# A hybrid decoder layer on one core: decay tiles clamped on ScalarE, running sums two ticks later, two mix tiles split together

## The chip, the core and the metric

The kernel runs on one core of a Trainium2 chip. A core has a matrix engine (PE, with its weight loads PEld), a vector engine (DVE), a scalar engine (ACT), GpSimd (POOL) and SyncE (SP, which here only issues DMAs). Each engine executes its own instructions in the order in which they are written, and waits on semaphores for the others. The metric is the device time of one execution in microseconds; the times shown are medians over several runs.

## The reference

One layer is computed for 256 tokens of width 1024, in float32:

```
p = x @ W_in -> [z | xBC | dt | q | k | v | gates]
s = Mamba-2 SSD mixer(z, conv(xBC), dt)      # 32 heads of 64, 4 groups, state 128
a = sliding-window attention with sinks(q, k, v)
m = (sig(g_s) * (s @ P_ssm) + sig(g_a) * (a @ P_attn)) @ W_o
h = LayerNorm1(alpha * x + m)
y = LayerNorm2(alpha * h + MoE(h))           # top 4 of 32 experts
```

The part that the change touches most is the decay inside one chunk of 128 tokens. With the running sums `a_cum = cumsum(dt * A)` of each head, it is

```
seg    = a_cum[:, :, :, None] - a_cum[:, :, None, :]
decay  = exp(where(causal, seg, -inf))
y_diag = einsum('bctgn,bcsgn->bctsg', C, B) * decay @ (x * dt)
```

## The kernel before, in words

**Front, 0 to 402 us.** All projections run here. Each weight tile is 128 x 2048 floats (1 MB). SP loads it into one of two ring slots (`load_raw`, L110). ACT copies it to a rounded high part (`act`, L67), DVE subtracts to get the low part (`sub_lo`, `tt`, L70), and PE makes three passes: high by high, high by low and low by high (`mm3`, L81). One half of a tile (128 output columns by 256 tokens) is 24 matmuls and one tick of the kernel's own clock. `take()` hands out the next tile; before that, `split_ahead` splits the tiles that come `st["la"]` places later: first the ACT copies, then all work that has fallen due (`run_due`), then the DVE subtractions. A ring slot is free again when the DVE subtraction has read it.

**Order of the side work.** `later(d, fn)` puts work d ticks ahead; generators that `yield need(d, ...)` are resumed when their tick has come and their counters allow. So the constants DT, DD and DE and the number in each `later` set where an instruction stands in its engine's queue. The tiles come in the order k, v, c8 to c11 (convolved B and C), then q0, c0, c1, q1, and so on, then z, the gates, the output projections and four mix tiles.

**Running sums.** `part_dt` issues `dt_product` (the dt projection), one tick later `dt_chain` (softplus by a series on DVE; result `av` = dt * A; transposes `pdn` at L404), DD ticks later `decays` (the sums `pacum` by matmul with triangles, then `acn`, `eac`, `dte` on ACT), and one tick after that `decay_rows`: PE transposes `acn` to `acT` (L515), ACT copies it and sends it to memory as `accd` (L518).

**Decay tiles.** `ssd(c, g)` runs for two chunks and four groups. It loads a tile E of 128 x 8 x 128 (the sums of 8 heads, spread over all partitions) from `accd` through POOL's queue (L525). For each head DVE subtracts that head's own sum and takes the minimum with zero (`ts`, L75, 8 instructions). One tick later ACT takes Exp of the whole tile; a tick after that DVE multiplies by the masked C-B product; then 16 matmuls per pair of groups form `yd` with E as their weights. `xs` and `xd` are scaled copies of the transposed conv output; their DVE instructions free the PSUM banks in which PE's `ws` sums go on.

**Mix and experts.** The last output projection tiles (`yss`) are gated into `m`; `mix(c, q)` multiplies by the four mix tiles. Then come LayerNorm 1, the router and, from 401.6 us, the experts: a stream of 2 MB tiles, issued by `prefetch` (L140) on SP into ten slots that the front's weight tiles use as well. An expert tile waits for its slot's last reader.

Of the kernel before, what the change touches and what calls it, by code (L numbers as in the profile page):

```python
# [11 lines left out]
AF = mybir.ActivationFunctionType  # L12
OP = mybir.AluOpType
AX = mybir.AxisListType

P = 128
# [15 lines left out]
SILU = "silu_and_others"  # L32
OVER, AL = 27, 7
BIAS = 12 * 18 + 4
DT, DD, DE = 2, 4, 2
D3 = 4
L1 = 2
LG, LS = 1, 1
# [6 lines left out]
def hybrid_layer(ctx, tc, x, w_in, conv_w, conv_b, dt_bias, a_log, d_skip, norm_w, w_ssm_out,  # L45
# [10 lines left out]
    def ptile(name, dt=F):  # L56
        return gran.tile([P, 4096], dt, name=name, tag="g")
# [5 lines left out]
    def bank(name):  # L63
        return psum.tile([P, 512], F, name=name, tag="bank")

    def act(o, i, func=AF.Copy, **kw):
        return nc.scalar.activation(o, i, func, **kw)  # L67

    def tt(o, a, b, op):
        return nc.vector.tensor_tensor(o, a, b, op=op)  # L70

    def ts(o, a, s1, s2, op0, op1=None):
        if op1 is None:
            return nc.vector.tensor_scalar(o, a, s1, None, op0=op0)  # L74
        return nc.vector.tensor_scalar(o, a, s1, s2, op0=op0, op1=op1)  # L75
# [4 lines left out]
    def mm(o, l, r, start, stop):  # L80
        return nc.tensor.matmul(o, l, r, start=start, stop=stop)  # L81
# [16 lines left out]
    st = {"dma": 0, "split": 0, "la": 1}  # L98
# [33 lines left out]
    def prefetch(upto):  # L132

        while moe[0] < min(upto, len(stream) - S_E):
            m = moe[0]
            ap, nb = stream[S_E + m]
            t = ptile(f"w{m}").rearrange("p (k n) -> p k n", n=nb)
            last = S_E + m == len(stream) - 1
            for ks in (slice(0, 2), slice(2, 3), slice(3, 4)) if last else (slice(0, 4096 // nb),):
                nc.sync.dma_start(t[:, ks], ap[:, ks])  # L140
            raws[S_E + m] = t
            moe[0] += 1
# [7 lines left out]
    def later(d, fn):  # L150
        due.setdefault(clock[0] + d, []).append(fn)
# [6 lines left out]
    def weights(i):  # L158

        prefetch_raw()  # L160
        split_ahead(i)
        prefetch_raw()
        nb = stream[i][1]
        return tuple(t.rearrange("p (k n) -> p k n", n=nb) for t in splits.pop(i))
# [67 lines left out]
    def w2(shape, name):  # L232
        return work.tile(shape, F, name=name, tag="w2", bufs=TB["w2"])

    def w4(shape, name):
        return work.tile(shape, F, name=name, tag="w4", bufs=TB["w4"])

    def sm(name, n=64, dt=F):
        return work.tile([P, n], dt, name=name, bufs=1)
# [65 lines left out]
    def need(d, when=None, **n):  # L305

        return clock[0] + d, when, n

    def done(**n):
        for k, v in n.items():  # L310
            left[k] += v
# [19 lines left out]
    def tick(end):  # L331
        clock[0] += 1
        if end:
            pend[0] = True
        else:
            run_due()
            side()

    def side():
        owed[0] = min(owed[0] + st.get("rate", 0), 4)  # L340
        while owed[0] >= 1 and advance():
            owed[0] -= 1

    def mm3(o, hi, lo, s, ah, al, first=True, last=True):

        for k in range(8):
            mm(o, hi[:, k, s], ah[:, k], first and k == 0, False)
            mm(o, hi[:, k, s], al[:, k], False, False)
        for k in range(8):
            mm(o, lo[:, k, s], ah[:, k], False, last and k == 7)  # L350
# [3 lines left out]
    def take():  # L354
        nxt[0] += 1
        w = weights(nxt[0] - 1)
        if pend[0]:
            pend[0] = False
            side()
        return w  # L360
# [26 lines left out]
    def dt_product():  # L387
        pdt = bank("pdt")
        for k in range(8):
            mm(pdt[0:32, 0:NT], wdth[:, k], xh[:, k], k == 0, False)  # L390
            mm(pdt[0:32, 0:NT], wdth[:, k], xl[:, k], False, False)
            mm(pdt[0:32, 0:NT], wdtl[:, k], xh[:, k], False, k == 7)
        pc = bank("pc")
        nc.tensor.transpose(pc[:, 0:120], cnat[0:120], ident[0:120, 0:120])
        nc.tensor.transpose(pc[:, 128:144], gnat, ident[0:16, 0:16])
        act(ccol[:, 0:120], pc[:, 0:120], scale=0.5)
        act(gcol, pc[:, 128:144], scale=0.5)
        ts(dtT, pdt[0:32, 0:NT], dtb[:, 0:1], None, OP.add)
# [80 lines left out]
    Bn, cbm, c1 = cb_t[:, 0], [cb_t[:, 1], cb_t[:, 2]], cb_t[:, 3]  # L479
# [20 lines left out]
    acn = sm("acn")  # L500
# [19 lines left out]
    def ssd(c, g):  # L520
        gcs = slice(512 * g, 512 * g + 512)
        yield need(0, w4=1, xe=1 - c)
        E = w4([P, 8, P], "E")
        r = 32 * c + 8 * g
        nc.gpsimd.dma_start(E, accd[r:r + 8].unsqueeze(0).to_broadcast([P, 8, P]))  # L525
        if c == 0:
            xe = w2([P, 512], "xe")
            nc.gpsimd.tensor_tensor(xe.rearrange("p (h d) -> p h d", d=64),
                                    xs[0][:, gcs].rearrange("p (h d) -> p h d", d=64),
                                    dte[:, 8 * g:8 * g + 8].unsqueeze(2).to_broadcast([P, 8, 64]), op=OP.mult)  # L530
        yield need(DE)
        for h in range(8):
            ts(E[:, h], E[:, h], acn[:, r + h:r + h + 1], 0.0, OP.subtract, OP.min)
        later(1, lambda: act(E, E, AF.Exp))
        later(2, lambda: tt(E, E, cbm[c][:, g, None, :].to_broadcast([P, 8, P]), OP.mult))
        yield need(1, (lambda: g in ready) if c else None, bank=1)
        if c == 0:
            pst = bank(f"st{g}")
            mm(pst, Bn[:, g], xe, True, True)

        else:
            po = bank(f"yo{g}")
            mm(po, c1[:, g], xs[0][:, gcs], True, True)

            def ev():
                tt(po.rearrange("p (h d) -> p h d", d=64), po.rearrange("p (h d) -> p h d", d=64),
                   eac[:, 8 * g:8 * g + 8].unsqueeze(2).to_broadcast([P, 8, 64]), OP.mult)
                tt(xd[1][:, gcs], po, xd[1][:, gcs], OP.add)
                done(bank=1)
            later(1, ev)  # L550
        yield need(2, bank=1)
        py = bank(f"yd{c}{g}")
        for h in range(8):
            mm(py[:, 64 * h:64 * h + 64], E[:, h], xs[c][:, 512 * g + 64 * h:512 * g + 64 * h + 64], True, True)

        def add_y():
            tt(xd[c][:, gcs], py, xd[c][:, gcs], OP.add)
            done(bank=1, w4=1)
            ready.add((c, g))
            if c == 0:  # L560
                act(xs[0][:, gcs], pst)
                later(1, lambda: ready.add(g))
                done(bank=1, xe=1)
        later(1, add_y)
# [146 lines left out]

    def part_dt():
        dt_product()
        later(1, dt_chain)
        later(DD, decays)
        later(DD + 1, decay_rows)

    for kind, j in ORDER:
        if kind == "c":
            conv(j)  # L720
            if j == 11:
                start(3, prep())
            elif j < 8 and j % 2:
                start(5, ssd(0, j // 2), ssd(1, j // 2))
# [71 lines left out]
    def bias_cols():  # L796
        pg = bank("pgu")
        for b in range(16):
            o = 512 * (b // 4 % 2) + b % 4
            nc.tensor.transpose(pg[:, 32 * b:32 * b + 32], bgn[b // 8][:, o:o + 509:4], ident[0:32, 0:32])  # L800
        pg3 = pg.rearrange("p (b e) -> p b e", e=32)
        act(bgu[:, 0:8], pg3[:, 0:8])
        ts(bgu[:, 8:16], pg3[:, 8:16], 1.0, None, OP.add)
# [3 lines left out]
    def merge(blk, ps):  # L807
        t = w1([P, NT], "mg")
        stt(t, gts[0][:, blk], 1.0, ps, OP.add, OP.mult)
        tt(mrg[:, blk], mrg[:, blk], t, OP.add)  # L810
        act(mh[:, blk], mrg[:, blk], scale=0.5)
        stt(ml[:, blk], mrg[:, blk], 0.5, mh[:, blk].bitcast(F), OP.mult, OP.subtract)

    st["la"] = LS
    for n in range(4):
        if n == 1:
            prefetch(2)
            nc.scalar.preload_act_table_set(EXP_LN)
        ps = [bank(f"yss{n}{b}")[:, 0:NT] for b in range(2)]
        for kh in range(2):  # L820
            hi, lo = take()
            if n == 3 and kh == 1:
                st["la"] = 2
            for b in range(2):
                mm3(ps[b], hi, lo, slice(b * P, (b + 1) * P), *yT[kh], kh == 0, kh == 1)
                if kh:
                    later(1, lambda b=b, n=n, ps=ps: merge(2 * n + b, ps[b]))
                tick(b == 1)
            if n == 0 and kh == 0:
                bias_cols()  # L830
# [417 lines left out]
    scale = []  # L1248
# [40 lines left out]
```

## Time and profile before

| | us |
|---|---|
| median of 3 runs | 1321.22 (1319.17 to 1322.77) |
| the profiled execution | 1322.42 |
| its span in the trace | 1320.6 |
| PE busy | 1242.5 (94%) |
| DVE busy | 432.7 (33%) |
| ACT busy | 282.7 (21%) |
| POOL busy | 22.3 (2%) |

The shares are means over two very different parts. In the front all of PE, DVE and ACT have much to do and wait for each other. In the expert stage, which takes two thirds of the span, DVE and ACT are nearly idle and the DMA share is about 1. A wait or a busy share is therefore to be read in its own stretch. PEclk is the clock that TensorE was granted, 1.00 being the upper of its two levels (2.4 GHz) and 0.5 the lower (1.2 GHz); a mean between them says that part of the stretch ran at each.

### The profile page before, as it was taken

What the parts mean: (1) busy time and instruction counts of PE and PEld (TensorE: products, weight loads), DVE (VectorE), ACT (ScalarE), POOL (GpSimd) and SP (SyncE); (2) the same over time, 40 slices, a digit from 0 to 9 for tenths busy, and PEclk for the clock granted to TensorE, in tenths of its full rate; (3) what the DMA queues carried; (4) which work ended last, traced back from release to release, by engine and by line L of the source; (5) the groups of instructions that cost most, each with busy time, mean ns of one, the idle gap of its engine ahead of it and who ended that gap; (6) DMA issues with size and microseconds to landing.
All of it is one profiled execution on the core that took longest, in us unless ns stands there. A gap on an engine that the chain in (4) does not pass through costs nothing. (4 is left out here: it accounts for less than half of the span.)

```text
span 1320.6 us, 16115 instructions
## 1 busy us (share of the span) xinstructions
PE 1242.5 (94%) x6835; PEld 676.4 (51%) x6835; DVE 432.7 (33%) x877; ACT 282.7 (21%) x471; POOL 22.3 (2%) x28
## 2 busy tenths in 40 slices
PE   7998899999999999999999999898999989879995
PEld 7997777999874343443433334243333424333331
DVE  4899878664651121112111121111111211111114
ACT  3655545653411110111100101010110101000001
POOL 0001101000000000000000000000000000000000
PEclk9999989999999999999999999999999999989998
DMA  6544345667598999999999999999999999999994
GB/s 207 161 154 157 115 140 188 224 219 276 191 430 337 430 430 431 431 430 430 431 429 430 432 429 430 432 430 429 431 432 428 431 431 430 431 426 431 431 429 173
DMA packets 80002, 467.49 MB, mean 354 GB/s; under 512 B 7052, under 2 KB 46164, under 8 KB 55220
## 3 DMA queue, kind: packets, MB, share of 16 engines
q1 hardware_dynamic: 78500, 460.99, 85.0%
q0 software_dynamic: 1200, 4.33, 0.9%
q8 instruction: 55, 0.90, 0.2%
q10 hardware_dynamic: 224, 1.08, 0.2%
q14 instruction: 23, 0.19, 0.0%
HBM read 465.30 MB, written 1.08 MB: 353 GB/s over the span
## 5 line engine op out<-in xcount | busy, mean ns | idle before, releaser
L81 PE MATMUL u<-w,xg 128*64 128x512 f32 x2048 | 462.5, 596 | 20.1 <-DMA w<-in_w_gate_up_dram 20.0
L81 PEld LDWEIGHTS u<-w,xg 128*64 128x64 f32 x2048 | 140.1, 137 | 310.7 <-issue 260.8
L81 PE MATMUL d<-w,ac 128*64 128x512 f32 x1024 | 241.2, 602 | 19.2 <-DVE gg L75 9.0
L1052 DVE COPY gu<-u 128x512 f32<-128x512 f32 x32 | 22.1, 692 | 678.8 <-PE u L81 678.8
L81 PE MATMUL ws<-x,w 128*128 128x256 f32 x1200 | 158.7, 293 | 5.4 <-DVE xd L70 3.2
L81 PEld LDWEIGHTS ws<-x,w 128*128 128x128 f32 x1200 | 151.9, 199 | 9.1 <-issue 5.1
L81 PEld LDWEIGHTS d<-w,ac 128*64 128x64 f32 x1024 | 68.4, 137 | 141.8 <-issue 123.4
L70 DVE TENSOR_TENSOR w<-ring,w 128x2048 fp32r<-128x2048 f32 (+1 forms) x51 | 115.4, 2268 | 32.3 <-ACT w L67 32.2
L67 ACT ACTIVATE w<-ring 128x2048 fp32r<-128x2048 f32 (+1 forms) x51 | 95.6, 1878 | 73.3 <-DMA ring<-in_w_in_dram 19.0
L67 ACT ACTIVATE gu<-u 128x512 f32<-128x512 f32 x32 | 19.1, 597 | 320.1 <-PE u L81 320.1
L81 PEld LDWEIGHTS xg<-G,single 128*128 128x128 f32 x512 | 62.8, 196 | 25.0 <-issue 24.3
L81 PE MATMUL xg<-G,single 128*128 128x128 f32 x512 | 68.9, 288 | 0.5 <-DVE G L70 0.5
L67 ACT ACTIVATE xg<-xg 128x512 f32<-128x512 f32 x32 | 19.1, 597 | 218.1 <-PE xg L81 218.1
L81 PE MATMUL out<-y,S 64*128 64x512 f32 x256 | 63.6, 615 | 0.8 <-ACT y L67 0.8
L67 ACT ACTIVATE hg<-hg 128x512 f32<-128x512 f32 x32 | 20.2, 632 | 148.0 <-DVE hg L74 148.0
L81 PE MATMUL z<-w,x 128*128 128x512 f32 x192 | 49.4, 411 | 0.0
L81 PE MATMUL yss<-yt,w 128*128 128x256 f32 x384 | 47.0, 284 | 0.2 <-DVE w L70 0.2
L81 PEld LDWEIGHTS yss<-yt,w 128*128 128x128 f32 x384 | 46.3, 192 | 0.8 <-DVE w L70 0.4
L1063 PEld LDWEIGHTS tu<-ident,gu 128*128 128x128 f32 x256 | 33.4, 210 | 25.5 <-issue 24.3
L81 PEld LDWEIGHTS out<-y,S 64*128 64x128 f32 x256 | 22.0, 186 | 41.9 <-issue 40.2
L70 DVE TENSOR_TENSOR hg<-tu,bgu 128x256 f32<-128x256 f32 x64 | 26.9, 420 | 48.7 <-PE tu L1063 48.5
L67 ACT ACTIVATE y<-d 128x512 f32<-128x512 f32 x32 | 19.1, 597 | 105.5 <-PE d L81 105.5
(214 smaller groups left out, 805.6 us busy)
## 6 DMA issues: line engine op xcount, KB each, us to landing
w<-in_w_gate_up_dram SPq DMA_DIRECT2D x128, 2048.0 KB, 38.6
w<-in_w_down_dram SPq DMA_DIRECT2D x63, 2048.0 KB, 38.8
ring<-in_w_in_dram SPq DMA_DIRECT2D x33, 1024.0 KB, 5.1
ring<-in_w_ssm_out_dram SPq DMA_DIRECT2D x8, 1024.0 KB, 6.6
E<-accd POOLq DMA_DIRECT2D x8, 512.0 KB, 5.0
ring<-in_w_attn_out_dram SPq DMA_DIRECT2D x4, 1024.0 KB, 5.1
ring<-in_w_mix_out_dram SPq DMA_DIRECT2D x4, 1024.0 KB, 7.7
single<-in_x_dram SPq DMA_DIRECT2D x2, 512.0 KB, 3.7
```

The costliest lines, as they stand in the source:

```text
L67: return nc.scalar.activation(o, i, func, **kw)
L70: return nc.vector.tensor_tensor(o, a, b, op=op)
L81: return nc.tensor.matmul(o, l, r, start=start, stop=stop)
L1052: nc.vector.tensor_copy(t, banks[hf])
L1063: nc.tensor.transpose(pb[:, b], gu[hf][:, b:b + 509:4], ident)
```

## The change

Four edits:

- In `ssd` the eight DVE instructions per E (subtract, minimum) are replaced by eight ACT instructions, Relu with scale -1 and the head's sum as bias, and Exp takes scale -1, so that the same exp(min(x - a, 0)) results. The Exp follows at once rather than a tick later, and DVE's multiplication comes one tick earlier. 64 instructions move from DVE to ACT.
- `dt_chain` comes two ticks after `dt_product`, not one.
- DD is 6, not 4: `decays` and `decay_rows` come two ticks later.
- Before the second half of the last output tile (n = 3, kh = 1) is taken, `st["la"]` becomes 2, so that mix tiles 0 and 1 are both split there; and the third expert tile is allocated and issued there (`prefetch(3)`).

```diff
--- before.py
+++ after.py
@@ -32,7 +32,7 @@
 SILU = "silu_and_others"
 OVER, AL = 27, 7
 BIAS = 12 * 18 + 4
-DT, DD, DE = 2, 4, 2
+DT, DD, DE = 2, 6, 2
 D3 = 4
 L1 = 2
 LG, LS = 1, 1
@@ -530,9 +530,9 @@
                                     dte[:, 8 * g:8 * g + 8].unsqueeze(2).to_broadcast([P, 8, 64]), op=OP.mult)
         yield need(DE)
         for h in range(8):
-            ts(E[:, h], E[:, h], acn[:, r + h:r + h + 1], 0.0, OP.subtract, OP.min)
-        later(1, lambda: act(E, E, AF.Exp))
-        later(2, lambda: tt(E, E, cbm[c][:, g, None, :].to_broadcast([P, 8, P]), OP.mult))
+            act(E[:, h], E[:, h], AF.Relu, scale=-1.0, bias=acn[:, r + h:r + h + 1])
+        act(E, E, AF.Exp, scale=-1.0)
+        later(1, lambda: tt(E, E, cbm[c][:, g, None, :].to_broadcast([P, 8, P]), OP.mult))
         yield need(1, (lambda: g in ready) if c else None, bank=1)
         if c == 0:
             pst = bank(f"st{g}")
@@ -711,7 +711,7 @@
 
     def part_dt():
         dt_product()
-        later(1, dt_chain)
+        later(2, dt_chain)
         later(DD, decays)
         later(DD + 1, decay_rows)
 
@@ -818,9 +818,11 @@
             nc.scalar.preload_act_table_set(EXP_LN)
         ps = [bank(f"yss{n}{b}")[:, 0:NT] for b in range(2)]
         for kh in range(2):
+            if n == 3 and kh == 1:
+                st["la"] = 2
             hi, lo = take()
             if n == 3 and kh == 1:
-                st["la"] = 2
+                prefetch(3)
             for b in range(2):
                 mm3(ps[b], hi, lo, slice(b * P, (b + 1) * P), *yT[kh], kh == 0, kh == 1)
                 if kh:
```

How the edits move instructions shows best at three places. The first is ACT's queue where the running sums are evicted (28 to 60 us); w_472, w_540 are the splits of weight tiles 6 and 7, sz and cacc belong to the convolution.

```order
 L67 ACTIVATE w_472<-ring 128x2048
+L67 ACTIVATE sz<-cacc 128x256
+L67 ACTIVATE cacc<-ws,ccol 128x256
+L67 ACTIVATE sz<-cacc 128x256
+L67 ACTIVATE cacc<-ws,ccol 128x256
+L67 ACTIVATE w_540<-ring 128x2048
 L67 ACTIVATE acn<-pacum 128x64
 L67 ACTIVATE eac<-pacum 128x32
```

Before, acn followed the split of tile 6 and tile 7's split (w_552 by the old numbering) came after acT. Now two more pairs of conv work and the split of tile 7 stand ahead of acn.

The second place is the first pair of E, near 120 us, on DVE. Before:

```order
L75 TENSOR_SCALAR E<-E,acn 128x128 x16
L70 TENSOR_TENSOR xs<-xb_0_1343,dtv 128x256
L70 TENSOR_TENSOR xd<-xb_0_1343,dsk 128x256
L70 TENSOR_TENSOR xs<-xb_1_1348,dtv 128x256
L70 TENSOR_TENSOR xd<-xb_1_1348,dsk 128x256
L78 SCALAR_TENSOR_TENSOR cacc<-ws,ccol,cacc 128x255
L78 SCALAR_TENSOR_TENSOR cacc<-ws,ccol,cacc 128x254
L78 SCALAR_TENSOR_TENSOR cacc<-ws,ccol,cacc 128x253
L70 TENSOR_TENSOR w_1341<-ring,w_1341 128x2048
L78 SCALAR_TENSOR_TENSOR xc<-xc,cacc 128x256
L70 TENSOR_TENSOR E<-E,qcb 128x1024 x2
```

and after the change:

```order
L70 TENSOR_TENSOR xs<-xb_0_1345,dtv 128x256
L70 TENSOR_TENSOR xd<-xb_0_1345,dsk 128x256
L70 TENSOR_TENSOR xs<-xb_1_1350,dtv 128x256
L70 TENSOR_TENSOR xd<-xb_1_1350,dsk 128x256
L70 TENSOR_TENSOR E<-E,qcb 128x1024 x2
L78 SCALAR_TENSOR_TENSOR cacc<-ws,ccol,cacc 128x255
L78 SCALAR_TENSOR_TENSOR cacc<-ws,ccol,cacc 128x254
L78 SCALAR_TENSOR_TENSOR cacc<-ws,ccol,cacc 128x253
L70 TENSOR_TENSOR w_1343<-ring,w_1343 128x2048
L78 SCALAR_TENSOR_TENSOR xc<-xc,cacc 128x256
```

xb_0 and xb_1 are transposed conv blocks; E<-E,qcb is the multiplication. The sixteen clamps are gone from DVE, xs and xd move to the front, and the multiplications come ahead of the next taps and the next weight tile. The clamps stand on ACT, at the same place:

```order
 L67 ACTIVATE w_1245<-ring 128x2048
 L67 ACTIVATE qcb<-ws 128x256
-L67 ACTIVATE cacc<-ws,ccol 128x256 x2
-L67 ACTIVATE w_1341<-ring 128x2048
-L67 ACTIVATE xc<-cacc 128x256
-L67 ACTIVATE E<-E 128x1024 x2
+L67 ACTIVATE cacc<-ws,ccol 128x256
+L67 ACTIVATE E<-E,acn 128x128 x8
+L67 ACTIVATE E<-E 128x1024
+L67 ACTIVATE E<-E,acn 128x128 x8
+L67 ACTIVATE E<-E 128x1024
+L67 ACTIVATE cacc<-ws,ccol 128x256
```

The split of the next tile (w_1341 before, w_1343 now) stands behind sixteen clamps and two Exp.

The third place is the mix, on DVE; w_3443 is the last output tile, w_3500 and w_3502 are mix tiles 0 and 1, and mg, gate and m are the gating of the last output block.

```order
 L70 TENSOR_TENSOR w_3443<-ring,w_3443 128x2048
 L70 TENSOR_TENSOR w_3500<-ring,w_3500 128x2048
+L70 TENSOR_TENSOR w_3502<-ring,w_3502 128x2048
 L78 SCALAR_TENSOR_TENSOR mg<-gate,yss_3441 128x256
 L70 TENSOR_TENSOR gate<-gate,mg 128x256
 L78 SCALAR_TENSOR_TENSOR m<-gate,m 128x256
 L74 TENSOR_SCALAR ia<-ident 128x128
```

The subtraction of mix tile 1 now stands ahead of the gating; before, it came after the last m.

## Rows read from the trace of the kernel before

**Rows 1.** Busy time of engines in stretches around the start of the expert stage.

```profile
core 0: us, PE busy (x) PEld busy (x) DVE busy (x) ACT busy (x) POOL busy (x), PEclk, DMA share, GB/s
400.00:407.00 7.00, 7.00 (x41) 3.41 (x41) 1.11 (x8) 2.78 (x5) 0.00 (x0) 1.00 0.26 47
407.00:1294.00 887.00, 848.37 (x4068) 325.60 (x4064) 134.02 (x352) 88.75 (x157) 0.30 (x1) 1.00 1.01 430
```

**Rows 2.** Timeline (start us, duration us, engine, line, operation) at the first u matmuls.

```profile
401.61 8.80 PE L81 MATMUL u<-w,xg 128*64 128x512 f32 x40
...
405.31 3.76 SPq L140 DMA_DIRECT2D w<-in_w_gate_up_dram  x2
```

**Rows 3.** Waits of PE, 0 to 402 us: total us, times, longest us.

```profile
PE yd L81 <- DVE E L70: 4.9, 2, 3.7
...
PE ws L81 <- DVE xd L70: 3.2, 1, 3.2
...
PE pacum L81 <- DVE av L78: 1.9, 1, 1.9
```

**Rows 4.** Busy time of engines in three stretches of the front.

```profile
52.00:112.00 60.00, 59.45 (x515) 57.98 (x515) 57.29 (x103) 36.22 (x77) 5.21 (x5) 1.00 0.53 163
116.00:140.00 24.00, 18.48 (x129) 16.96 (x129) 19.83 (x41) 9.97 (x15) 1.65 (x2) 0.86 0.42 137
156.00:176.00 20.00, 15.77 (x82) 13.38 (x80) 17.00 (x39) 7.87 (x11) 2.55 (x3) 0.83 0.41 131
```

**Rows 5.** Groups of ACT by form, 0 to 402 us: count, busy us, mean ns, idle.

```profile
L67 ACT ACTIVATE E<-E 128x1024 f32<-128x1024 f32 x8 | 8.5, 1058 | 10.7 <-DVE E L75 8.3 <-issue 2.4
...
L67 ACT ACTIVATE sc<-sc,mx 128x128 f32<-128x128 f32 x16 | 6.2, 396 | 0.0
...
L67 ACT ACTIVATE acn<-pacum 128x64 f32<-128x64 f32 x1 | 0.2, 208 | 0.0
```

**Rows 6.** Timeline, clamps of two E on DVE.

```profile
119.01 3.22 DVE L75 TENSOR_SCALAR E<-E,acn 128x128 f32<-128x128 f32 x16
```

**Rows 7.** Timeline, 42 to 62 us.

```profile
42.18 4.52 PE L81 MATMUL ws<-x,w 128*128 128x256 f32 x24
...
44.10 2.28 DVE L70 TENSOR_TENSOR w<-ring,w 128x2048 fp32r<-128x2048 f32 x1
...
47.17 15.00 PE L81 MATMUL ws<-x,w 128*128 128x256 f32 x123
...
52.05 1.90 ACT L67 ACTIVATE w<-ring 128x2048 fp32r<-128x2048 f32 x1
```

**Rows 8.** DMA issues of the page: KB each, median us from issue to landing.

```profile
ring<-in_w_in_dram SPq DMA_DIRECT2D x33, 1024.0 KB, 5.1
```

**Rows 9.** Timeline, 114 to 141 us; in brackets idle time before, and its releaser.

```profile
114.31 1.02 ACT L67 ACTIVATE cacc<-ws,ccol 128x256 f32<-128x256 f32 x2
...
123.04 4.60 PE L81 MATMUL ws<-x,w 128*128 128x256 f32 x24 [3.17 <-DVE xd L70]
...
128.80 1.97 PE L81 MATMUL yd<-xs,E 128*128 128x64 f32 x16 [1.16 <-DVE E L70]
...
130.58 4.61 PE L81 MATMUL ws<-x,w 128*128 128x256 f32 x24
...
137.21 3.13 PE L81 MATMUL ws<-x,w 128*128 128x256 f32 x24
```

**Rows 10.** Timeline, 164 to 173 us.

```profile
164.95 3.65 PE L81 MATMUL yd<-xs,E 128*128 128x64 f32 x16 [3.70 <-DVE E L70]
...
168.36 4.54 PE L81 MATMUL z<-w,x 128*128 128x512 f32 x12
```

**Rows 11.** Timeline, mix matmuls, 356 to 373 us.

```profile
356.73 2.91 PE L81 MATMUL mix<-w,m 128*128 128x512 f32 x12
...
360.43 0.49 PE L81 MATMUL mix<-w,m 128*128 128x512 f32 x1 [0.79 <-ACT w L67]
...
362.75 9.59 PE L81 MATMUL mix<-w,m 128*128 128x512 f32 x34 [1.83 <-DVE w L70]
```

## Prediction

> **What bounds the kernel now.** I read the table of stretches first, from the end of the kernel backwards. From 407 to 1294 us the DMA share is 1.01: the expert stage runs at the speed at which weights arrive. In the 7 us ahead of that the share is only 0.26, with PE busy throughout [rows 1]. The timeline there says why: the eleventh expert tile is issued at 405.31, in the middle of the first run of u matmuls, which began at 401.61; ten tiles are resident and it waits for a slot that PE empties [rows 2]. So the long stretch hangs on one moment, the first u matmul. What makes that moment earlier takes the same time off the end. What only loads expert tiles earlier lengthens the empty stretch and gains nothing. The change can act through the front alone.
>
> In the front I list what PE waits for. Long ones are yd for the decay tile E, ws for xd and pacum for av [rows 3]; at the end mix waits for its weight tile, for ACT's half of it and for DVE's. From 52 to 112 us PE is busy 59.45 of 60 us: whatever delays PE before 52 stays. Around E, in 116 to 140 and 156 to 176, PE is idle 5.5 and 4.2 us, with a mean clock of 0.86 and 0.83 [rows 4]; a wait is paid there twice, as a wait and as matmuls at the lower of the two clock levels after it.
>
> **The price of the new ACT work.** No row shows a Relu of 128x128. The nearest ACT rows are acn, 128x64, 208 ns, below, and sc, 128x128, which also reads an accumulator, 396 ns, above; Exp over a whole E takes 1058 ns [rows 5]. I take the middle, 0.30 us: 8 relus 2.4 us, with Exp 3.5 us per E (bounds 2.7 and 4.2), and 64 x 0.30 = 19 us more on ACT in all. DVE loses the same 64; sixteen of them took 3.22 us, 201 ns each [rows 6], so 13 us.
>
> The Trainium skill (ScalarE: Activation LUTs, "Rules for kernel authors") sends relu to VectorE, not to ScalarE; by its figures an ACTIVATE with a pointer bias and 128 columns would follow the last after some 294 ns, an estimate. That gives 2.35 us per E, and the sum would stay. The 201 ns of DVE agree with the rule that the same work is dearer on ACT; here it is a question of which of the two is waited for.
>
> **Running sums two ticks later (zone A, 28 to 60 us).** Before, pacum waits 1.85 us for av, and the 24 ws matmuls behind it take 4.52 us, where the 123 from 47.17 take 15.00, or 2.93 for 24 [rows 3, 7]. With two more ticks between, DVE has the sums in time: 1.85 + 1.6 = 3.4 us gained. But acn now stands behind the split of w_540 in ACT's queue, and acT, which needs acn, stands in PE's queue between the two halves of c11. That split needs its raw tile, whose ring slot comes free when DVE has subtracted w5. Before, that ended at 44.10 + 2.28 = 46.4; after, DVE has the same work ahead of it and a short wait for sp_u, which stands behind a split on ACT: about 47.3. A ring load lands in 5.1 us [rows 8], so ACT starts at 52.4 (before: 52.05), needs 1.9 us, and acn and acT come at about 54.6. Before, c11's halves ended at 47.17 + 2 x 2.93 = 53.0 and at 56.0; PE, 3.4 us ahead, is through the first at about 49.6. So PE meets **a new wait of about 5 us at acT**, perhaps with a slow group behind it (1.6 us): c11 ends at 57.8 to 59.4, 1.9 to 3.4 us later than before. Behind acT on PE stand c11's second half and the q tile; behind the split on ACT stand the next evictions of conv sums, for which DVE has work of its own until about 57. The copy of acT to memory moves by some 7 us, and nothing loads from it in this zone. PE is full to 112, so the delay travels, less the 0.5 us of idle time there [rows 4]. Zone A: **2.5 us lost**, bounds 0 (if the raw tile lands early) and 4.
>
> **Decay tiles, chunk 0 (zone B).** Before, ws waits 3.17 us for xd, which is queued on DVE behind the sixteen clamps of 119.01; yd waits 1.16 for E; and two groups of ws run at 4.60 and 4.61 us where the next takes 3.13 [rows 9]. After, xd follows the taps at once. ACT has its cacc of 114.31 done before 116 and needs 7 us for two E, which puts the multiplications at about 123, where PE comes to yd. The xd wait shrinks to about 0.5 and yd's goes: 2.7 + 1.2 = 3.9 us. The two slow groups hold 2.9 us over the fast one; pt still waits for cacc in front of them, so I count 1.6. **5.5 us gained**, bounds 3.5 and 7.
>
> **Decay tile at 160 (zone C).** yd waits 3.70 us for an E that is clamped, exponentiated and multiplied with DVE's and ACT's other work between. Then yd takes 3.65 us (1.97 near 129 [rows 9]) and z 4.54, where the ratio of the ws groups would make it 3.1 [rows 10]. After, ACT can clamp as soon as E is there and DVE multiply without the taps between, near 161, when PE is there (164.95 - 3.70): 3.7 us of wait, and up to 1.7 + 1.4 = 3.1 of clock, of which I count 2.3. The next E is loaded by POOL, and its relus hold ACT until it lands, with the split of the next weight tile behind them; for that I take off 0.5. **5.5 us gained**, bounds 3.5 and 7. The later four E lie in a stretch where PE waits for nothing; what ACT gets there is covered by its own idle time.
>
> **Mix tiles and third expert tile (zone D).** mix waits 0.79 us for ACT's split and 1.83 for DVE's of the second mix tile [rows 11]. Split one tile earlier, its low part is there at about 358, and the last m, which it pushes back, at about 361.3, just when PE wants it. Saved: 2.6 us, and some of the slower clock behind it (34 mix matmuls took 9.59 us; the twelve at 356.73 took 2.91, so 34 would take 8.2); I take 0.4. **3.0 us gained**, bounds 1.5 and 4. The third expert tile only has another slot to wait for, and what waits behind it on SP is expert tiles. They come some 2.5 us sooner, which is worth nothing by itself [rows 1, 2].
>
> **Sum.** 5.5 + 5.5 + 3.0 - 2.5 = 11.5 us off the first u matmul (401.6 to about 390) and off the end. The profiled execution took 1322.42 us, 1.2 above the median shown: 1310.9 there, 1309.7 against the median, so 1310.
>
> **Rivals.**
> 1. The clock stays low: PE still idles a little around E (pt for cacc), the groups behind stay slow, and zone A pays its slow group. Then B 3.9, C 3.2, D 2.6, A -4: 5.7 us, 1315.5. For it: a wait of 1.85 us was enough at 41 us. Against it: less is idle in sum.
> 2. PE waits for ACT where it waited for DVE. With relus at 396 ns, the first Exp pair is done near 124.7 and the multiplications near 127; PE, ready at 123.4, waits 3.7 us at yd. B is then worth 1.7, C 1.0, D 3.0, A -2.5: 3.2 us, 1318, no change that can be told. For it: the only 128x128 row of ACT is that one. Against it: that row also reads an accumulator.
> 3. Slower: ACT executes in order, and a relu waits for its E's load where a DVE clamp did before; ACT's splits of the next weight tiles stand behind. Eight E are loaded. Once each costs PE on average (11.5 + 4) / 8 = 1.9 us more than counted, the kernel is slower by 4: 1325, and 3 us more each make it 1334. For it: it is ACT's split, and DVE's after it, that mix waits for at 360 us [rows 11]. Against it: PE uses a tile several us after its split, and ACT was busy only 36 of 60 us from 52 to 112 and less than half around E [rows 4]. The rule of the Trainium skill above (ScalarE: Activation LUTs) belongs to this rival: it would hold if ACT were the engine waited for.
>
> **Chances.** Forecast 0.62, its own range 1305 to 1314. Rival 1 0.17, rival 2 0.13, rival 3 0.08. A measurement of this kernel tells 0.3% (4 us) from no change. Rival 1 lies mostly beyond that (0.14 to 0.03), rival 2 mostly within (0.11 to 0.02): faster 0.78, within 0.14, slower 0.08. The bounds of the terms sum to 1303 (18 off) at the low end; the high end reaches through rival 2, 1318.5.
>
> **What would show it.** Right: no ws wait for xd and no yd wait for E of over 1 us; a mean clock over 0.95 in the stretches of [rows 4]; a new acT wait for acn of some 5 us near 50; no mix wait; the first u matmul near 390 and the same time from there to the end. Wrong: if the end comes earlier by another amount than the first u matmul, the reading of the expert stage falls; if acT waits under 3 us, zone A; if yd waits for E with ACT's Exp just ahead of it, the price of the relus.

## The result and the profile after

The changed kernel takes 1311.1 us (median of 4 runs, 1309.95 to 1311.2); the kernel before took 1321.99 us in the same session (4 runs). The ratio is 0.9919, with a 95% interval of 0.9902 to 0.9936: 10.9 us less, of 11.5 forecast. The profiled execution took 1311.2 us, its span is 1309.4 (before: 1320.6).

The end first. Timeline of the changed kernel (start us, duration us, engine, line, operation), at the first u matmuls; it answers to [rows 2]:

```profile
390.89 8.80 PE L81 MATMUL u<-w,xg 128*64 128x512 f32 x40
...
394.58 3.76 SPq L140 DMA_DIRECT2D w<-in_w_gate_up_dram  x2
```

The first u matmul comes 10.7 us earlier, and the eleventh expert tile is still issued 3.7 us behind it. From there to the end of the span it is 918.5 us, before 919.0. The 883 us from 400 us on are as full of DMA as before [rows 1] (busy time by engine, then granted clock, DMA share, GB/s):

```profile
400.00:1283.00 883.00, 844.85 (x4051) 324.68 (x4050) 133.95 (x352) 88.68 (x157) 0.29 (x1) 0.99 1.01 430
```

So all but 0.5 us of the gain arises ahead of 391 us. What PE waits for there (releaser: total us, times, longest), against [rows 3]:

```profile
PE acT L515 <- ACT acn L67: 5.9, 1, 5.9
...
PE ao L81 <- ACT sc L67: 1.8, 1, 1.8
PE pt L615 <- DVE cacc L78: 1.2, 1, 1.2
...
PE pt L615 <- DVE xd L70: 1.0, 1, 1.0
PE yt L682 <- DVE xd L78: 0.9, 1, 0.9
```

The waits of yd for E, of ws for xd, of pacum for av and of mix for its tile are gone. One long wait is new, at acT, and a short one at ao, for ACT's copy of sc. The waits of pt and yt for xd have each grown by 0.7 us (0.3 and 0.2 before); that of pt for cacc is as it was. The stretches of [rows 4]:

```profile
52.00:112.00 60.00, 58.62 (x487) 57.18 (x488) 55.07 (x95) 33.34 (x71) 5.21 (x5) 0.94 0.51 159
...
116.00:140.00 24.00, 20.93 (x169) 17.93 (x167) 21.84 (x32) 19.18 (x39) 4.37 (x3) 1.00 0.48 159
...
156.00:176.00 20.00, 18.60 (x111) 14.08 (x111) 17.06 (x32) 13.64 (x24) 3.23 (x2) 1.00 0.56 184
```

Around E PE is idle 3.1 and 1.4 us instead of 5.5 and 4.2, at a granted clock of 1.00. From 52 to 112 us the mean clock fell from 1.00 to 0.94. ACT, the fourth figure, is now busy 19 of 24 us there; it was 10.

The running sums, 44 to 65 us, against [rows 7]:

```profile
44.38 3.11 PE L81 MATMUL ws<-x,w 128*128 128x256 f32 x24
...
51.30 1.91 ACT L67 ACTIVATE w<-ring 128x2048 fp32r<-128x2048 f32 x1 [0.61 <-DMA ring<-in_w_in_dram]
...
53.38 0.42 PE L515 MATMUL acT<-ident,acn 128*64 128x128 f32 x1 [5.88 <-ACT acn L67]
...
53.45 10.83 PE L81 MATMUL ws<-x,w 128*128 128x256 f32 x69
```

PE is through c11's first half at 47.5, then stands until ACT has split tile 7 (ACT, held up by DVE before that, waits another 0.61 us for the ring load); 69 matmuls behind it take 10.83 us, 2.4 more than at the 2.93 for 24 of [rows 7]. The first pair of E, against [rows 6, 9]:

```profile
117.02 2.45 ACT L67 ACTIVATE E<-E,acn 128x128 f32<-128x128 f32 x8
...
122.17 3.10 PE L81 MATMUL ws<-x,w 128*128 128x256 f32 x24
...
122.61 1.21 DVE L70 TENSOR_TENSOR E<-E,qcb 128x1024 f32<-128x1024 f32 x1
...
124.10 1.23 DVE L70 TENSOR_TENSOR E<-E,qcb 128x1024 f32<-128x1024 f32 x1 [0.28 <-ACT E L67]
...
125.11 1.90 PE L81 MATMUL yd<-xs,E 128*128 128x64 f32 x16
...
131.76 1.63 PE L81 MATMUL ao<-sc,single 128*64 128x256 f32 x12 [1.76 <-ACT sc L67]
...
146.25 1.90 PE L81 MATMUL yd<-xs,E 128*128 128x64 f32 x16
```

Each E has 16 yd matmuls of its own (the trace has 128 for the eight E), not 16 for a pair. The yd at 125.11 reads the first E, multiplied by 123.8: no wait, and 1.3 us to spare. The second E, whose multiplication begins 0.1 us after its Exp on ACT, is read only at 146.25. A wait of 1.76 us at ao is new. The E near 160, against [rows 10]:

```profile
157.83 1.91 PE L81 MATMUL yd<-xs,E 128*128 128x64 f32 x16
...
163.33 2.45 ACT L67 ACTIVATE E<-E,acn 128x128 f32<-128x128 f32 x8 [1.74 <-DMA E<-accd]
...
166.56 3.03 PE L81 MATMUL z<-w,x 128*128 128x512 f32 x12
```

yd waits for nothing, though its E was multiplied only 0.2 us earlier (156.42 to 157.62); the relus of the next E wait 1.74 us for its load. And the mix, against [rows 11]: 96 matmuls in one run.

```profile
349.23 21.95 PE L81 MATMUL mix<-w,m 128*128 128x512 f32 x96
```

The starts of a few PE instructions place the gains; the table is worked out from the timelines of all kernels. A is the start of the first `st` (chunk states, near 113 us); B is from there to the second `st`, C to the third, then to the first `yt`, to the first mix matmul, to the first u matmul, and to the end of the span.

```
                     A      B     C   to yt to mix to u  | u at   span
before             113.3  40.9  45.0  64.5  93.0  44.9  | 401.6  1320.6
changed            115.6  35.4  38.8  65.2  94.3  41.7  | 390.9  1309.4
changed, again     115.6  35.4  40.4  65.1  94.6  42.8  | 393.8  1313.1
e1 relu only       112.5  35.4  38.8  65.7  94.6  44.9  | 391.8  1310.4
e2 sums only       117.1  39.4  43.5  64.2  93.2  44.9  | 402.3  1321.0
e3 mix only        111.7  39.4  44.8  64.3  93.3  38.4  | 391.8  1310.6
e4 no third tile   116.8  35.4  38.8  65.1  94.3  41.8  | 392.1  1311.1
e5 acT later       114.3  35.4  40.4  65.3  94.3  41.4  | 391.1  1309.8
e6 relu twice      116.8  41.0  42.1  73.6  94.2  41.8  | 409.6  1328.7
e7 DVE clamps      114.2  38.4  42.0  64.9  94.3  41.6  | 395.6  1314.6
e8 relu and mix    113.0  35.4  40.4  65.4  94.5  41.6  | 390.3  1309.6
e8 again           112.5  35.4  40.4  65.3  94.4  42.8  | 390.9  1309.6
e9 sums one later  111.6  35.4  40.4  65.3  94.4  41.3  | 388.4  1307.1
```

Between the two kernels of the comparison: A 2.3 us later, B 5.5 shorter, C 6.2 shorter, 0.7 and 1.2 longer up to the mix, 3.2 shorter from the mix on.

### The profile page after: what moved, and what is told of

It is laid out like the page before. It is cut to its first block, busy times and chain, and to the rows that moved or that the text cites. A ratio compares the mean times of both kernels' runs of the same rounds, so it can differ in the third digit from the quotient of the medians.

```text
span 1309.4 us, 16114 instructions
## 1 busy us (share of the span) xinstructions
PE 1237.4 (95%) x6835; PEld 673.5 (51%) x6835; DVE 421.5 (32%) x813; ACT 300.0 (23%) x535; POOL 23.7 (2%) x28
```

## The experiments

Each ratio is against the kernel before on the same chip, with its 95% interval. Each run has one profile; its row is in the table (the changed kernel and e8 were run twice).

**Each edit alone.** e1 makes the first edit alone (clamps as Relu on ACT, Exp at once, multiplication a tick earlier).

> Only the clamps move from DVE to ACT, with the Exp at once and the multiplication a tick earlier. Theory (parts add up): the trace of the changed kernel puts zones B and C at 5.5 and 6.2 us, so about 11.5 us faster than before, near 1310.5; the waits of ws for xd and of yd for E are gone, the acT wait of 5.9 us is not there, the mix waits are. Rival (the parts lean on each other: PE comes to zone B 2.3 us earlier than with the later sums, and DVE and ACT are not earlier): part of the gain of B comes back as waits there, 7 to 9 us faster, 1313 to 1315.

1310.98 us, ratio 0.9929 (0.9915 to 0.9942): 8.9 us. B and C are as in the changed kernel, so they don't need the later sums, and the rival's waits in B are not there. The time stands with the first expectation, but the gain with the second: the interval (7.7 to 11.2 us) leaves 11.5 just outside. What is missing went behind C: 1.2 and 1.5 us up to the mix. e2 makes the second and third:

```diff
-DT, DD, DE = 2, 4, 2
+DT, DD, DE = 2, 6, 2
-        later(1, dt_chain)
+        later(2, dt_chain)
```

> Only the running sums come two ticks later. Theory: PE waits about 5.9 us at acT and arrives 2.3 us late at 112 us; all of it stays, first u matmul near 404, about 2.3 us slower, 1324. Rival (before, PE waits for DVE's xd and E in zone B anyway, so a late PE loses nothing): no change, first u matmul at 401.6, PE's xd wait near 123 shorter by some 2 us.

1323.61 us, ratio 1.0029 (1.0018 to 1.0041): slower by 3.7 us. Waits of PE in its trace:

```profile
PE acT L515 <- ACT acn L67: 5.9, 1, 5.9
PE yd L81 <- DVE E L70: 4.4, 2, 3.7
...
PE ws L81 <- DVE xd L70: 3.2, 1, 3.2
```

The acT wait is there, and the xd wait is not shorter by it: when PE is late, DVE is late too. e3 makes the fourth:

```diff
             for kh in range(2):
+                if n == 3 and kh == 1:
+                    st["la"] = 2
                 hi, lo = take()
                 if n == 3 and kh == 1:
-                    st["la"] = 2
+                    prefetch(3)
```

> Only the last edit: mix tiles 0 and 1 split together, third expert tile issued there. Theory: 3.0 us faster, first u matmul near 398.5, no mix wait, 1319. Rival (the two waits only move to the m tiles that stand behind the second subtraction on DVE): 0 to 1 us.

1314.83 us (7 runs, 1312.4 to 1317.95), ratio 0.9967 (0.9954 to 0.9980): 4.4 us by the ratio (2.6 to 6.1), 3.0 expected, and no mix wait. The profiled run is the fastest of them: in it the clock did not fall between mix and u (38.4 us in the table), and in the other profiles this stretch is 2.9 us longer or more. The router's matmuls behind the mix show it, first in e3, then in the changed kernel:

```profile
383.11 1.95 PE L81 MATMUL lg<-wr,hT 128*128 128x32 f32 x16
...
385.12 1.96 PE L81 MATMUL out<-single,ia 128*128 128x512 f32 x4
```

```profile
378.98 3.08 PE L81 MATMUL lg<-wr,hT 128*128 128x32 f32 x16
...
382.30 3.76 PE L81 MATMUL out<-single,ia 128*128 128x512 f32 x4
```

Together the three come to 8.9 + 4.4 - 3.7 = 9.6 us; the changed kernel measured 10.9 and, in a later session, 7.3.

**The third expert tile.**

```diff
-            if n == 3 and kh == 1:
-                prefetch(3)
```

> The changed kernel without its prefetch(3). Theory: as the changed kernel, 1311, first u matmul near 390.9; expert tiles start later and the empty stretch ahead of the eleventh tile is shorter, nothing else. Rival (the earlier stream counts): about 2 us slower than the changed kernel, 1313.

1311.15 us, ratio 0.9931 (0.9917 to 0.9945). The run of tiles is issued 0.9 us after the first mix matmul rather than 0.2, and from the first u matmul to the end it is 919.0 us. The earlier tile is worth nothing that can be told.

**Engine or order in time.** e7 keeps the new order and puts the clamps back on DVE.

```diff
-            act(E[:, h], E[:, h], AF.Relu, scale=-1.0, bias=acn[:, r + h:r + h + 1])
-        act(E, E, AF.Exp, scale=-1.0)
+            ts(E[:, h], E[:, h], acn[:, r + h:r + h + 1], 0.0, OP.subtract, OP.min)
+        act(E, E, AF.Exp)
```

> The changed kernel with the clamps on DVE as before, but the Exp at once and the multiplication one tick later as in the change. Theory: both count: ws waits for xd behind sixteen clamps as before (3 us and slow clock after it), while the waits of yd for E go: about half of the gain of B and most of C stay, 1314 to 1315. Rival (only the order in time counts): 1311. Rival (only the engine counts): 1320 and more.

1317.85 us, ratio 0.9981 (0.9972 to 0.9989): 2.5 us faster than before, and by the ratios 5 to 8 us slower than the changed kernel (0.9945 and 0.9919), between the first expectation and the last. Timeline at the first pair of E:

```profile
119.93 3.21 DVE L75 TENSOR_SCALAR E<-E,acn 128x128 f32<-128x128 f32 x16
...
123.96 5.04 PE L81 MATMUL ws<-x,w 128*128 128x256 f32 x24 [3.17 <-DVE xd L70]
```

With the clamps on DVE the xd wait is back to the hundredth, 3.17 us, and so is a slow group behind it. Against e2 and e3 the order in time gives 1 us in B and 1.5 to 3 in C; the rest of B and C is the engine.

**Is there room on ACT?** e6 adds a second relu that changes nothing.

```diff
             act(E[:, h], E[:, h], AF.Relu, scale=-1.0, bias=acn[:, r + h:r + h + 1])
+            act(E[:, h], E[:, h], AF.Relu)
```

> The changed kernel with each relu followed by a second one that changes nothing: 2.4 us more of ACT per E, 19.5 us in all. Theory: ACT has no room left for E in zones B and C, yd waits for E there: 3 to 4 us in B, 2 in C, and the slower clock behind the waits; the later four E are covered: 5 to 8 us slower than the changed kernel, 1316 to 1319. Rival (ACT is covered everywhere): 1311. Rival (ACT is the bound everywhere): 19 us slower, 1330.

Ratio 1.0065 (1.0052 to 1.0078), against 0.9919 to 0.9945 for the changed kernel: 16 to 19 us slower than that, the last of the three expectations; the theory fell here. In the trace a pair takes 0.63 us where a single relu took 0.31, so each E costs 2.6 us more, 21 in all. Waits of PE from 112 to 300 us, and the second E on DVE:

```profile
PE ws L81 <- DVE cacc L78: 5.4, 1, 5.4
PE yo L81 <- ACT xs L67: 3.3, 1, 3.3
PE yd L81 <- DVE E L70: 2.9, 2, 2.2
PE ao L81 <- ACT sc L67: 2.3, 2, 1.9
```

```profile
130.79 1.23 DVE L70 TENSOR_TENSOR E<-E,qcb 128x1024 f32<-128x1024 f32 x1 [4.93 <-ACT E L67]
...
133.59 0.77 PE L81 MATMUL ws<-x,w 128*128 128x256 f32 x2 [5.35 <-DVE cacc L78]
```

DVE stands 4.93 us at the second E's multiplication, and the taps behind it, which have nothing to do with E, come late to PE. The yd of the first E waits for nothing here, and PE reads the second E only at 153.14: an E that nothing needs yet holds PE up, by way of DVE's queue. In C yd does wait, 2.2 us. Even the last four E, which I took as covered, cost 8.4 us more (column to yt). Of the ACT time added, 5.2 us in B, 5.2 in C and 10.4 up to yt, PE lost 5.7, 3.3 (1.8 against the repeat) and 8.4: ACT has little room in any stretch with an E.

**Is it acT?** e5 puts acT where PE does not wait for it.

```diff
-        later(DD + 1, decay_rows)
+        later(DD + 3, decay_rows)
```

> The changed kernel with decay_rows two ticks later (DD + 3), so that acT no longer stands in PE's queue between the halves of c11. Theory: the acT wait of 5.9 us and the slow clock behind it go, part of it comes back as a wait for a weight tile or for sz near 60 to 70 us, since DVE is full there; the stretch to the second xb is 3 to 4 us shorter: 1307 to 1308. Rival (DVE bounds this stretch, not acT): the wait only changes its name, 1310 to 1311.

1310.97 us, ratio 0.9920 (0.9907 to 0.9934): no gain that can be told. The acT wait fell to 0.3 us, but A came only from 115.6 to 114.3. Waits of PE in e5, and 60 to 112 us in e5:

```profile
PE xb L455 <- DVE xc L78: 2.1, 2, 1.2
...
PE ws L81 <- DVE w L70: 1.6, 2, 1.0
...
PE s L81 <- DVE cacc L78: 0.9, 1, 0.9
PE cb L81 <- DVE sz L78: 0.8, 1, 0.8
```

```profile
60.00:112.00 52.00, 48.08 (x408) 45.30 (x407) 49.41 (x88) 29.66 (x68) 5.21 (x5) 1.00 0.53 163
```

DVE, the third figure, is busy 49.4 of 52 us and PE 48.1; in the changed kernel it was 47.3 and 52.0. Most of the wait came back in pieces, at DVE.

**The sums in other places.** e8 leaves out the second and third edits (DD 4, chain one tick on).

> The changed kernel without its later sums (one tick for the chain, DD 4): clamps on ACT and the mix tiles. Theory (the later sums alone cost what they cost by themselves, 3 to 4 us): 1307 to 1308, the acT wait 2 us or less, zones B, C and D as in the changed kernel. Rival (with clamps on ACT the later sums cost nothing, since zone B takes the delay up): 1311.

1311.09 us, ratio 0.9925 (0.9912 to 0.9938), the same as the changed kernel, although its first `st` is 2.6 us earlier. Both were run again with e9, which also has the chain as before, but the sums one tick later:

```diff
-DT, DD, DE = 2, 4, 2
+DT, DD, DE = 2, 5, 2
```

> The changed kernel once more, on the same chip as its version without the later sums. Theory: 1311, the segments from pdt to u as in its first profile within 1 us, but for those in which the clock falls.

> The version without the later sums once more. Theory (the later sums cost 2.5 us before the first st, which the slow clock near 170 us gave back by chance in the one profile): 2 us or more faster than the changed kernel here, 1309. Rival (what it gains there is lost in zone C every time): the same time, and again the slow clock near 170 us.

> Clamps on ACT, mix tiles together, the chain one tick after the product as before, but DD 5: the sums one tick later, ahead of the split of tile 7 in ACT's queue. Theory (the later sums are worth their 3 us as long as acn does not stand behind that split): no pacum wait, no acT wait, second st near 110 us instead of 113 (sums as before) or 116 (sums of the change), 1308. Rival (DVE bounds the stretch to 112 us): st near 113, 1310 to 1311.

The changed kernel: 1311.91, ratio 0.9945 (0.9931 to 0.9958). e8 again: 1311.41, 0.9937 (0.9923 to 0.9951). e9: 1309.81, 0.9932 (0.9919 to 0.9946), between its two expectations; its first `st` is at 111.6, the earliest with clamps on ACT, and 3.3 us of acT wait are left, where the theory had none. The three intervals overlap: no version is shown to beat the changed kernel, and what the later sums cost in it, by the profiles 2.6 to 3 us, is not seen in its timed runs. The repeat shows one reason why such sums are hard to tell. The same z group of the same program (the first profile has it above at 166.56, 3.03 us) in the second profile of the changed kernel:

```profile
166.57 4.60 PE L81 MATMUL z<-w,x 128*128 128x512 f32 x12
```

The waits ahead of it are the same to 0.01 us. From 166.0 to 171.3 us the granted clock was 1.00 in the first profile and 0.68 in the second. The slow clock came in one execution and not in the other: 1.6 us.

## Why the prediction was right, and where not

- **The sum, 11.5 us.** Measured 10.9 in one session and 7.3 (5.5 to 9.1) in the next; the edits alone add up to 9.6. That the first number comes so close is in part luck: 2.0 us lost between the third `st` and the mix were not forecast, and B and D reached their sizes by other terms than those counted.
- **The end hangs on the first u matmul.** Right: 918.5 to 919.4 us from there to the end in all thirteen profiles, whatever was changed ahead of it and whenever the expert stream began.
- **Zone A, 2.5 us lost.** The size was right (A 2.3 us later; e2 alone 3.7 slower), and so was the acT wait (5.9 us, 5 forecast), behind the split of tile 7. Both its ends came earlier than the sum has them: PE was through c11's first half at 47.5, not 49.6 (waits of 0.8 us at pdn and 0.4 at acT, which the sum left out, went too), and acT ran at 53.4, not 54.6. The slow group behind it cost 2.4 us and took the mean clock of 52 to 112 us to 0.94, just under the 0.95 that was to show the forecast right. "PE is full to 112, so the delay travels" was half of it: e5 takes 5.6 us of the wait away, and the first `st` comes only 1.3 us earlier, still 1.0 later than before, since DVE is nearly as full as PE there and becomes the one that is waited for.
- **Zone B, 5.5 us.** Measured 5.5, but from other terms than 3.9 of waits and 1.6 of clock. The waits for xd and E gave 4.3 and the two slow groups 3.0 (both take 3.1 us now). The new wait at ao took 1.8 back, which the sum doesn't have: PE comes there earlier, and the sc that it needs leaves ACT's queue hardly earlier than before (131.13, before 131.63), behind a wait of ACT for DVE's cacc. Of the clock, 1.5 us belong to a slow group that is not always there: B took 39.4 us in e2 and e3, whose code is as before there, and 40.9 in the one profile that I read, so 4.0 us are the change's. The mechanism held: the xd wait went with the sixteen clamps (e7), and the first E was done 1.3 us before PE came. The reading of yd was wrong in one point: it needs the first E alone, so rival 2, too, counted a wait for two E where PE needs one.
- **Zone C, 5.5 us.** Measured 6.2 in one profile and 4.7 in the other. The wait of 3.70 us went; yd and z gave 3.2 us of clock in the first and 1.7 in the second, 2.3 counted.
- **The price of a relu, 0.30 us.** Measured 2.45 us for 8, 0.306 each; the row below gives a mean of 392 ns, as successive instructions overlap. (Group of ACT: count, busy us, mean ns.)

```profile
L67 ACT ACTIVATE E<-E,acn 128x128 f32<-128x128 f32 x64 | 19.5, 392 | 1.7 <-DMA E<-accd 1.7
```

By the figures of the Trainium skill (ScalarE: Activation LUTs, "What ACT_TABLE_LOAD costs") the estimate was 294 ns from one to the next; the 306 measured agree. Its rule that relu goes to VectorE ("Rules for kernel authors") would have cost time here: e7, which keeps the clamps there, is 5 to 8 us slower.

- **"The later four E ... covered by its own idle time": wrong,** though it cost little here. The first yt came 0.7 us later, with a wait of 0.9 for xd; e6 shows that little is left there to cover more (8.4 of 10.4 us came through). PE's waiting for nothing in the profile before was no measure of how near ACT was.
- **Zone D, 3.0 us.** 3.2 from the mix to u, 2.1 in the repeat. The two mix waits went as forecast (2.6 us). The mix matmuls at the lower clock gave 2.1, not 0.4; 1.6 of that were lost again behind the mix, where the clock was 0.57 and 0.58 from 379 to 387 us. In e3 it stayed at 1.00 there, and D was 6.5 us. So the size was luck.
- **Ahead of the mix.** Not foreseen: 1.2 us lost in the output projections behind pgu, where the granted clock was 0.82 and 0.62 in two stretches of 3 us, with PE busy throughout. It is in all profiles with the new order of E, e7 too, and in none of before, e2 and e3. Why is open. Two stretches of the changed kernel, then the same place before:

```profile
306.00:309.00 3.00, 3.00 (x22) 2.96 (x22) 0.42 (x1) 1.57 (x2) 0.00 (x0) 0.82 0.89 309
309.00:312.00 3.00, 3.00 (x18) 3.00 (x18) 2.30 (x2) 0.61 (x1) 0.00 (x0) 0.62 0.00 0
```

```profile
315.00:318.00 3.00, 3.00 (x26) 2.96 (x26) 0.42 (x1) 1.73 (x2) 0.00 (x0) 1.00 0.81 284
318.00:321.00 3.00, 3.00 (x27) 3.00 (x27) 2.51 (x2) 0.46 (x1) 0.00 (x0) 1.00 0.00 0
```

- **The rivals.** The clock stayed at 1.00 around E in the first profile of the changed kernel, so the first rival did not come about there, though zone A did pay its slow group. In the repeat the mean clock from 156 to 176 us was 0.91, and the 7.3 us gained lie nearer to that rival's 5.7 than to 11.5. The second and third did not come about, but e6 shows how near they were: 2.6 us more per E turn some ten microseconds gained into some nine lost. The third's price (1.9 us more per E than counted) stood in the right place; its path was another in zone B, DVE's queue behind the multiplication rather than ACT's splits.

## What to carry to other kernels

Where two engines feed a third and both are nearly full, read which of them holds an unrelated instruction back: the clamps cost DVE 3.2 us, and PE lost 3.2 us at xd, which needs no clamp. A move to the other engine pays only as far as that engine has time left: here 21 us more on ACT cost 16 to 19 (e6), so double the moved work once to see how far that is. And a long new wait on PE is worth removing only if the engine behind it is not just as late.

## What was not expected of the hardware

- The clock fell in some executions of one program and not in others at the same place (z of 12: 3.03 and 4.60 us), so single profiles differ by steps of 1.5 us, and a difference of 2 us between zones needs more than one profile.
- A relu that reads what the one just ahead of it wrote does not overlap with it: in e6 it starts 0.03 us after the other's end. The next, on another head, starts 0.09 us before the end of the one ahead.

```profile
118.25 0.41 ACT L67 ACTIVATE E<-E,acn 128x128 f32<-128x128 f32 x1
118.69 0.31 ACT L67 ACTIVATE E<-E 128x128 f32<-128x128 f32 x1
118.91 0.39 ACT L67 ACTIVATE E<-E,acn 128x128 f32<-128x128 f32 x1
```
